# Interleaving the norms of a two-layer decoder trunk with its matmuls, on eight cores

## The chip, the cores and the metric

The kernel runs on the eight cores of one Trainium2 chip. Every core runs the same program on its share of the batch: one new sequence of 2048 tokens and 16 running sequences with 8 new tokens each, 2176 tokens in all. The metric is the device time of the slowest core, in microseconds (us).

Executions come in two states. In the fast state all cores have nearly the same span and clock, and the times of one kernel agree within some 0.3%. In the slow state the cores of one die, sometimes of both, show a lower granted TensorE clock and the time is several per cent longer.

## The reference, cut to what matters

```python
for i in range(DEPTH):                                   # 2 layers
    a = rmsnorm(h, norm_mix[i])
    u, bg, cg, v = split(a @ w_in[i])                    # 4 x 512 columns
    y_pool = pool_mixer(u) ; y_conv = bg * short_conv(cg * v)
    h = h + concat(y_pool, y_conv) @ w_out[i]
    m = rmsnorm(h, norm_mlp[i])
    h = h + relu(m @ w_up[i]) ** 2 @ w_down[i]           # 1024 -> 4096 -> 1024
    gate = sigmoid(rmsnorm(h, norm_ple[i]) @ w_ple_gate[i])
    h = h + gate * (p[i] @ w_ple_proj[i])
return rmsnorm(h, norm_f), new pool states, new conv states
# rmsnorm(x, g) = x * rsqrt(mean(x * x) + 1e-6) * g, in fp32
```

Of the kernel before, what the change touches and what calls it, by code (L numbers as in the profile page):

```python
# [126 lines left out]
def build():  # L127
# [25 lines left out]
    AW = 18944  # L153
    es = ExitStack()
    with es:
        sb = lambda name, shape, dt: es.enter_context(nc.sbuf_tensor(name, shape, dt))
        h = sb("h", [128, KT, NTOK], F32)
        ring = sb("ring", [128, 4, 8, 512], BF16)
        wple = sb("wple", [128, 2, D], BF16)
# [3 lines left out]
        EH = sb("EH", [128, DEPTH, 4, NSEQ * POOL_BUF], F32)  # L163
# [42 lines left out]
        ld_ch = [P.chan(f"ld{i}") for i in range(4)]  # L206
# [50 lines left out]
        SPSTG = 12288  # L257
        SCSTG = 14336
        VSTG = 15360
        vstg = af(VSTG, 128)  # L260
        vstgB = P.abuf()
# [7 lines left out]
        for l in range(DEPTH):  # L269
# [13 lines left out]
            stg = af(SCSTG + l * 512, 512)  # L283
            sB_ = P.abuf()
# [12 lines left out]
        xstgB = [P.abuf() for _ in range(4)]  # L297
        xstg = [af(XSTG + i * 1024, 1024) for i in range(4)]
        for ti, (toff, tw) in enumerate(TILES):
            nsub = tw // 128  # L300
            for s_ in range(nsub):
                src = x_p[toff + s_ * 128: toff + (s_ + 1) * 128, :] if toff < SEQ else x_s
                P.op("sp", lambda e, s_=s_, src=src: e.dma_start(out=xstg[s_], in_=src), writes=[xstgB[s_]], chan=ld_ch[s_])
            if nsub == 4:
                for k in range(KT):
                    b = next_bank()
                    for s_ in range(4):
                        P.op("pe", lambda e, b=b, s_=s_, k=k: e.transpose(out=psum[b][:, s_ * 128:(s_ + 1) * 128], in_=xstg[s_][:, k * 128:(k + 1) * 128], identity=ident[:]),  # L308
                             reads=[xstgB[s_], identB], writes=[psB[b]], signal=(s_ == 3))
# [6 lines left out]
            else:  # L316
                for kh in range(2):
                    b = next_bank()
                    for kk in range(4):
                        k = kh * 4 + kk  # L320
                        P.op("pe", lambda e, b=b, kk=kk, k=k: e.transpose(out=psum[b][:, kk * 128:(kk + 1) * 128], in_=xstg[0][:, k * 128:(k + 1) * 128], identity=ident[:]),
                             reads=[xstgB[0], identB], writes=[psB[b]], signal=(kk == 3))
# [4 lines left out]
        def norm_tile(ti, dst_ap_fn, dstB, gbase):  # L327
            toff, tw = TILES[ti]
            b = next_bank()
            for k in range(KT):  # L330
                q = st["sq"]
                st["sq"] = (q + 1) % 4
                P.op("act", lambda e, q=q, k=k: e.activation(out=sq[:, q, 0:tw], in_=h[:, k, toff:toff + tw], func=AF.Square),  # L333
                     reads=[hB[k][ti]], writes=[sqB[q]])
                P.op("pe", lambda e, q=q, k=k, b=b: e.matmul(psum[b][:, 0:tw], lhsT=ones[:], rhs=sq[:, q, 0:tw], start=(k == 0), stop=(k == KT - 1)),  # L335
                     reads=[sqB[q], onesB], writes=[psB[b]], signal=True)
            n_ = st["norm"]
            st["norm"] = 1 - n_
            P.op("act", lambda e, b=b, n_=n_: e.activation(out=rstd[:, n_, 0:tw], in_=psum[b][:, 0:tw], func=AF.Sqrt, scale=1.0 / D, bias=EPS),  # L339
                 reads=[psB[b]], writes=[rstdB[n_]])  # L340
            P.op("dve", lambda e, n_=n_: e.reciprocal(out=rstd[:, n_, 0:tw], in_=rstd[:, n_, 0:tw]),  # L341
                 reads=[rstdB[n_]], writes=[rstdB[n_]])
            for k in range(KT):
                P.op("dve", lambda e, k=k, n_=n_: e.scalar_tensor_tensor(out=dst_ap_fn(k), in0=h[:, k, toff:toff + tw], scalar=vcol(gbase + k),  # L344
                                                                         in1=rstd[:, n_, 0:tw], op0=ALU.mult, op1=ALU.mult),
                     reads=[hB[k][ti], rstdB[n_], vecB], writes=[dstB[k]])

# [35 lines left out]
        R_OFF = [17408, 17920, 18432]  # L383
# [5 lines left out]
        PT_OFF = 8704  # L389
        G_OFF = [12928, 13440]  # L390
        TMP_OFF = [13952, 14464]
        pT_t = ab(PT_OFF, 2176).rearrange("p (k n) -> p k n", k=2)
        nB = mB
        n_t = m_t
        pTB = [[P.abuf() for _ in TILES] for _ in range(2)]
        gB = [P.abuf() for _ in range(2)]
        tmpB = [P.abuf() for _ in range(2)]
        YFM_OFF = [0, 4096]
        YTM_OFF = [8192, 9216]
        yfmB = [[P.abuf() for _ in range(KT)] for _ in range(2)]  # L400
        ytmB = [P.abuf() for _ in range(2)]

        for l in range(DEPTH):
# [3 lines left out]
            def do_group(l, grp):  # L407
# [39 lines left out]
                for il, ti in enumerate(tl):  # L447
                    o, tw = lo(il)
                    norm_tile(ti, lambda k, o=o, tw=tw: a_t[:, k, o:o + tw], [aB[k][il] for k in range(KT)], V_NMIX + l * 8)

                slot_u = ws_take()
                slot_c = ws_take()
                slot_v = ws_take()
                slot_b = ws_take()
# [7 lines left out]
                def u_chunk(g):  # L462
# [13 lines left out]
                    for il in range(ntl):  # L476
                        b = inproj(slot_u, g, il)
# [72 lines left out]
                def cv_chunk(j):  # L550
# [13 lines left out]
                    for il in range(ntl):  # L564
                        o, tw = lo(il)
                        bc = inproj(slot_c, j, il)
# [4 lines left out]
                        bv = inproj(slot_v, j, il)  # L571
# [31 lines left out]
                def conv_z(j):  # L603
# [5 lines left out]
                    P.op("dve", lambda e: e.tensor_scalar(out=af(Z_OFF, n_), in0=af(coff + 2, n_), scalar1=vcol(cwb + 8), scalar2=vcol(V_CB + l * 4 + j),  # L609
                                                          op0=ALU.mult, op1=ALU.add),  # L610
# [8 lines left out]
                def b_chunk(j):  # L619
                    for il in range(ntl):  # L620
                        o, tw = lo(il)
                        bb = inproj(slot_b, j, il)
                        P.op("dve", lambda e, bb=bb, il=il: e.tensor_tensor(out=dense(mix_t[:, 4 + j, :], il), in0=ctok(Z_OFF, il, 0), in1=pview(bb, il), op=ALU.mult),  # L623
                             reads=[ZB, psB[bb]], writes=[mixB[4 + j][il]])

                u_chunk(0)
                u_chunk(1)
                pool_ew(0)
                pool_state(0)
                u_chunk(2)  # L630
                pool_ew(1)
                pool_state(1)
                u_chunk(3)
                ws_release(slot_u)
                pool_mm(0)
                pool_ew(2)
                pool_state(2)
# [230 lines left out]
```

## The kernel before, where the change touches it

The state `h` lies feature-major in SBUF: 8 blocks of 128 features, each 2176 tokens wide in fp32. Tokens are cut into five tiles, four of 512 prompt tokens and a narrow one of 128 sample tokens. Weights come through a ring of four 1 MB blocks. Each engine is given its work in the order in which the program issues it.

A norm is one function, called for one tile at a time. ScalarE squares a block, TensorE sums it over the features with a matrix of ones, ScalarE takes the square root, and VectorE makes a reciprocal and eight scalings:

```python
def norm_tile(ti, dst_ap_fn, dstB, gbase):
    b = next_bank()
    for k in range(KT):
        P.op("act", ... sq[q] = Square(h[:, k, tile]))
        P.op("pe",  ... matmul(psum[b], lhsT=ones, rhs=sq[q]))
    P.op("act", ... rstd = Sqrt(psum[b] / D + EPS))
    P.op("dve", ... rstd = reciprocal(rstd))
    for k in range(KT):
        P.op("dve", ... dst[k] = h[:, k, tile] * g[k] * rstd)
```

The stages follow one another, each with all its norms ahead of its matmuls:

```python
for ti, (toff, tw) in enumerate(TILES):        # x: 4 staging buffers, loaded, transposed into h
    ...
for l in range(DEPTH):
    for grp in GROUPS:                         # tiles [0, 1], [2, 3], and [4] (the samples)
        for ti in grp: norm_tile(ti, ...)      # mixer norm
        # body: projections u, C, v, B, with pooling and conv between them
        for c in range(KT):                    # output projection, h += ...
            for ti in grp: ...
    for ti in range(5): norm_tile(ti, ...)     # MLP norm of all tiles
    for q in range(4):                         # quarters of the 4096
        for c in range(KT):
            for ti in range(5): ...            # up projection, relu (fp32), square
        for c in range(KT):
            for ti in range(5): ...            # down projection, h += ...
    for ti in range(5): ...                    # load p through 4 buffers, transpose it
    for ti in range(5): norm_tile(ti, ...)     # gate norm of all tiles
    for c in range(KT):
        for ti in range(5): ...                # gate stage: 8 gate matmuls, 2 of p; h += sigmoid * product
for ti in range(5):
    norm_tile(ti, ...)                         # final norm
    ...                                        # transpose back, store through 2 buffers
```

## Time and profile before

| | before |
|---|---|
| times ahead of the prediction | median 2168.81 us of 4 runs (2003.60 to 2258.54) |
| the fast one of them | 2003.60 us |
| profiled run, slowest core | 1998.7 us |
| TensorE busy | 1737.0 us (87%) |
| VectorE, ScalarE busy | 1010.4 us (51%), 466.2 us (23%) |
| mean granted TensorE clock of the slowest core | 0.896 |

The prediction shows the page and the table of stages. In the views PE is TensorE and PEld its weight loads, DVE is VectorE, ACT is ScalarE, POOL is GpSimd and SPq is the queue of SyncE; L730 is a line of the kernel's file. In a timeline a line is the start, the duration, the engine, the source line, the operation, output and inputs, the shape, and how many; in brackets stands the idle time of that engine before it and what ended it. This is TensorE's timeline in the kernel before, where layer 0's gate stage begins with the transposes of p (line L730):

```profile
863.89 1.04 PE L730 MATMUL ps<-ident,pstg 128*128 128x128 f32 x8
868.23 0.30 PE L730 MATMUL ps<-ident,pstg 128*128 128x128 f32 x1 [3.29 <-DMA pstg<-pp]
```

Eight transposes take 1 us and then TensorE waits for the next loads, since a buffer is loaded again only when its transposes are done. The second view is the list of waits of SyncE's queue, which issues the loads of x, in the first 100 us of the kernel before (what waits, for what, us in total, times, longest):

```profile
SPq L797 <- PE ps L308: 48.0, 4, 14.1
...
```

The queue that should issue loads waits 48.0 us for transposes to free a buffer: load and transpose take turns.

### The profile page before, as it was taken

The page shows a single profiled execution, that of the slowest core. Times are in us where ns is not written, and L with a number is a line of the kernel's source. Part 1 is how long each engine was busy: PE and PEld are TensorE (multiplying, and loading weights), DVE is VectorE, ACT ScalarE, POOL GpSimd, SP SyncE. Part 2 cuts the span into 40 slices and gives each one's busy share as a digit, 9 for nine tenths or more (in the row PEclk, how much of TensorE's full clock was granted, in tenths as well). Part 3 has the DMA queues.
Part 4 walks back from the last instruction along what each step waited for, and adds up shares of the span by engine and source line. Part 5 has one row for each costly group of instructions (what it writes and reads, how often), then busy time and mean ns, then how long its engine had stood idle before and what let it go on. Part 6 is the DMA issues. An engine that isn't in the chain of part 4 may idle for free.

```text
span 1998.7 us, 25940 instructions; the slowest of 8 cores (1987.1 to 1998.7 us)
## 1 busy us (share of the span) xinstructions
PE 1737.0 (87%) x8557; PEld 825.4 (41%) x8557; DVE 1010.4 (51%) x1568; ACT 466.2 (23%) x942; POOL 68.4 (3%) x99
## 2 busy tenths in 40 slices
PE   3489887699999999967979887699999999978955
PEld 3234334244444444422424334344444444432433
DVE  1185755744443434429676665744344443429655
ACT  1220311430211203023241311420220303124242
POOL 1000001000000000000000000000000000000000
PEclk8689897699999999977989898689999999977965
DMA  9415246612212212220134326712122122110022
GB/s 199 110 22 85 43 60 97 94 22 43 43 22 43 43 22 42 43 56 0 22 56 66 55 41 100 118 22 43 22 43 43 25 40 43 22 35 1 1 84 95
DMA packets 87887, 103.10 MB, mean 52 GB/s; under 512 B 3790, under 2 KB 81966, under 8 KB 87728
## 3 DMA queue, kind: packets, MB, share of 16 engines
q0 software_dynamic: 76480, 76.81, 26.0%
q1 hardware_dynamic: 11280, 24.64, 3.9%
q8 instruction: 74, 1.21, 0.3%
q14 instruction: 53, 0.43, 0.1%
HBM read 168.61 MB, written 10.10 MB: 89 GB/s over the span
## 4 chain that ended last, share of the span: by engine, by line
PE 73%; DVE 16%; DMA 6%; issue 3%; ACT 1%; SPq 1%; DVEq 0%; ACTq 0%; POOLq 0%
PE ps L353 69%; DVE arena L344 7%; DVE rstd L341 5%; DMA arena<-x_p 2%; PE ps L335 2%; DVE arena L495 1%; DMA ring<-w_out 1%; PE ps L308 1%; DMA pstg<-pp 1%; ACT sq L333 1%; PE ps L730 1%; DVE arena L612 1%; PE ps L773 1%; DMA y_p<-arena 1%; DVE arena L572 0%
## 5 line engine op out<-in xcount | busy, mean ns | idle before, releaser
L353 PE MATMUL ps<-arena,ring 128*128 128x512 bf16 (+1 forms) x7680 | 1506.8, 356 | 56.7 <-DVE arena L344 37.7
L353 PEld LDWEIGHTS ps<-arena,ring 128*128 128x128 bf16 x7680 | 711.0, 101 | 833.4 <-issue 135.3
L698 DVE TENSOR_TENSOR arena<-arena 128x512 bf16<-128x512 f32 (+1 forms) x320 | 189.6, 611 | 278.5 <-ACT arena L696 278.5
L711 DVE TENSOR_TENSOR h<-h,ps 128x512 f32<-128x512 f32 (+1 forms) x320 | 188.9, 607 | 275.6 <-PE ps L353 275.5
L696 ACT ACTIVATE arena<-ps 128x512 f32<-128x512 f32 (+1 forms) x320 | 163.9, 532 | 674.0 <-PE ps L353 652.4
L333 ACT ACTIVATE sq<-h 128x512 bf16<-128x512 f32 (+1 forms) x280 | 131.9, 553 | 163.1 <-PE ps L335 163.1
L344 DVE SCALAR_TENSOR_TENSOR arena<-h,vec,rstd 128x512 bf16<-128x512 f32 (+3 forms) x280 | 166.3, 666 | 4.5 <-PE ps L335 0.9
L335 PE MATMUL ps<-sq,ones 128*128 128x512 bf16 (+1 forms) x280 | 114.6, 461 | 58.4 <-ACT sq L333 49.2
L341 DVE RECIPROCAL rstd<-rstd 128x512 f32<-128x512 f32 (+1 forms) x35 | 100.4, 2869 | 107.8 <-ACT rstd L339 107.8
L672 DVE TENSOR_TENSOR h<-h,ps 128x512 f32<-128x512 f32 (+1 forms) x80 | 48.6, 608 | 82.5 <-PE ps L353 80.3
L335 PEld LDWEIGHTS ps<-sq,ones 128*128 128x128 bf16 x280 | 28.4, 102 | 143.8 <-issue 138.8
L750 ACT ACTIVATE arena<-ps 128x512 f32<-128x512 f32 (+1 forms) x80 | 42.5, 533 | 113.1 <-PE ps L353 86.0
L495 DVE TENSOR_TENSOR arena<-arena 128x1038 f32<-128x1038 f32 (+7 forms) x60 | 60.2, 1003 | 15.8 <-ACT arena L478 12.1
L308 PE MATMUL ps<-ident,arena 128*128 128x128 f32 x128 | 27.1, 381 | 46.5 <-DMA arena<-x_p 46.5
L752 DVE TENSOR_TENSOR arena<-arena,ps 128x512 f32<-128x512 f32 (+1 forms) x80 | 48.5, 606 | 34.3 <-ACT arena L750 25.5
L773 PE MATMUL ps<-ident,arena 128*128 128x128 f32 x136 | 35.2, 410 | 30.0 <-DVE arena L344 30.0
L754 DVE TENSOR_TENSOR h<-h,arena 128x512 f32<-128x512 f32 (+1 forms) x80 | 49.0, 612 | 9.1 <-DVE arena L752 0.9
L314 DVE COPY h<-ps 128x512 f32<-128x512 f32 x16 | 11.1, 692 | 75.2 <-PE ps L308 75.2
L732 ACT ACTIVATE arena<-ps 128x512 bf16<-128x512 f32 (+1 forms) x20 | 10.3, 532 | 150.6 <-PE ps L730 91.7
L353 PE MATMUL ps<-arena,wple 128*128 128x512 bf16 (+1 forms) x160 | 44.4, 360 | 0.7 <-DVE arena L752 0.7
L623 DVE TENSOR_TENSOR arena<-arena,ps 128x512 bf16<-128x512 f32 (+1 forms) x40 | 23.8, 607 | 41.8 <-PE ps L353 40.8
L308 PEld LDWEIGHTS ps<-ident,arena 128*128 128x128 f32 x128 | 23.1, 200 | 50.4 <-issue 50.4
(72 smaller groups left out, 445.3 us busy)
## 6 DMA issues: line engine op xcount, KB each, us to landing
ring<-w_in POOLq DMA_DIRECT2D x24, 1024.0 KB, 10.6
ring<-w_up POOLq DMA_DIRECT2D x16, 1024.0 KB, 8.9
ring<-w_down POOLq DMA_DIRECT2D x16, 1024.0 KB, 8.2
ring<-w_out POOLq DMA_DIRECT2D x12, 1024.0 KB, 10.2
arena<-x_p SPq DMA_DIRECT2D x16, 512.0 KB, 10.4
y_p<-arena SPq DMA_DIRECT2D x16, 512.0 KB, 2.6
pstg<-pp SPq DMA_DIRECT2D x32, 128.0 KB, 2.4
ring<-w_gate POOLq DMA_DIRECT2D x4, 1024.0 KB, 8.4
```

The costliest lines, as they stand in the source:

```text
L308: P.op("pe", lambda e, b=b, s_=s_, k=k: e.transpose(out=psum[b][:, s_ * 128:(s_ + 1) * 128], in_=xstg[s_][:, k * 128:(k + 1) * 128], ident ...
L333: P.op("act", lambda e, q=q, k=k: e.activation(out=sq[:, q, 0:tw], in_=h[:, k, toff:toff + tw], func=AF.Square), reads=[hB[k][ti]], writes ...
L335: P.op("pe", lambda e, q=q, k=k, b=b: e.matmul(psum[b][:, 0:tw], lhsT=ones[:], rhs=sq[:, q, 0:tw], start=(k == 0), stop=(k == KT - 1)), re ...
L341: P.op("dve", lambda e, n_=n_: e.reciprocal(out=rstd[:, n_, 0:tw], in_=rstd[:, n_, 0:tw]), reads=[rstdB[n_]], writes=[rstdB[n_]])
L344: P.op("dve", lambda e, k=k, n_=n_: e.scalar_tensor_tensor(out=dst_ap_fn(k), in0=h[:, k, toff:toff + tw], scalar=vcol(gbase + k), in1=rstd ...
L353: P.op("pe", lambda e, b=b, lap=lap, rap=rap, i=i: e.matmul(psum[b][:, 0:width], lhsT=lap, rhs=rap, start=(i == 0), stop=(i == n - 1)), re ...
L495: P.op("dve", lambda e, doff=doff, src_off=src_off, v=v, sh=sh: e.tensor_tensor(out=af(doff + v, EW - v), in0=af(src_off + v, EW - v), in1 ...
L696: P.op("act", lambda e, b=b, ri=ri, tw=tw: e.activation(out=af(R_OFF[ri], tw), in_=psum[b][:, 0:tw], func=AF.Relu), reads=[psB[b]], writes ...
L698: P.op("dve", lambda e, ri=ri, c=c, toff=toff, tw=tw: e.tensor_tensor(out=f_t[:, c, toff:toff + tw], in0=af(R_OFF[ri], tw), in1=af(R_OFF[r ...
L711: P.op("dve", lambda e, b=b, c=c, toff=toff, tw=tw: e.tensor_tensor(out=h[:, c, toff:toff + tw], in0=h[:, c, toff:toff + tw], in1=psum[b][ ...
L754: P.op("dve", lambda e, gi_=gi_, c=c, toff=toff, tw=tw: e.tensor_tensor(out=h[:, c, toff:toff + tw], in0=h[:, c, toff:toff + tw], in1=af(T ...
L773: P.op("pe", lambda e, b=b, kk=kk, k=k, yoff=yoff, s_=s_: e.transpose(out=psum[b][:, kk * 128:(kk + 1) * 128], in_=af(yoff + k * 512 + s_ ...
```

## The change

Its intent is that no norm stands alone on the path: each one is cut into pieces that are issued between the matmuls of something else. VectorE's nine steps of a norm go into a queue (`defer`), a step or two of which is issued after each matmul unit (`pump`; a unit is the matmuls that sum into one PSUM bank, and in the gate stage the two groups of one output block); `drain` issues what is left when the result is needed. In parts:

1. x is loaded through eight staging buffers, in two alternating sets of four.
2. The mixer norm of the second prompt group: squares and sums beside the first group's last B projections, scalings between its output projections.
3. The sample group's norm goes ahead of the second group's output projection.
4. The first quarter of the up projection goes tile by tile; only the norms of tiles 0 and 1 are summed ahead of it, those of tiles 2 to 4 beside it.
5. p is loaded and transposed behind each tile of that quarter.
6. The last down projection goes tile by tile, with the gate norm of the tile before beside it.
7. The gate stage goes tile by tile. In layer 0 it carries the sums of layer 1's first norm; in layer 1 the final norm, in place in `h`, with transposes and stores a tile later.
8. The first conv term moves from VectorE to ScalarE.
9. The relu result and its square's inputs are bf16, and so is the pool state.

The rest of the diff moves buffers to make room for this.

The core of the diff, with cuts marked:

```diff
-        xstgB = [P.abuf() for _ in range(4)]
+        xstgB = [P.abuf() for _ in range(8)]
+            xo = (ti % 2) * 4
...
-            for grp in GROUPS:
-                do_group(l, grp)
+            gs = [do_group(l, grp) for grp in GROUPS]     # (norm, body, output projection, scalings)
+            gs[0][0]()
+            gs[1][3](gs[0][1](GROUPS[1]["tiles"]))
+            gs[0][2](1)
+            for t_ in GROUPS[1]["tiles"]:
+                drain(t_, V_NMIX + l * 8)
+            gs[1][1]()
+            gs[2][0]()
+            gs[1][2]()
+            gs[2][1]()
+            gs[2][2]()
...
+                if q == 0:
+                    mlp_norm(0)
+                    N = norm_sums(1)
+                    defer(N, ...)
+                    for ti in range(NTL):
+                        drain(ti, V_NMLP + l * 8)
+                        N = norm_begin(ti + 2) if ti + 2 < NTL else None
+                        for c in range(KT):
+                            if N and c >= 4:
+                                norm_sq(N, [2 * (c - 4), 2 * (c - 4) + 1])
+                            up_unit(su, c, ti)
+                            pump(2 if c in (2, 3) else 1)
+                            if N and c >= 4:
+                                norm_mm(N)
...
+                        p_transposes([ti])
...
+                    prev = None                            # last down projection
+                    for ti in [4, 0, 1, 2, 3]:
+                        for c in range(KT):
+                            dn_unit(sd, c, ti)
+                            pump(2)
+                        if prev is not None:
+                            ple_norm(prev)
+                        prev = ti
...
+            for ti in range(NTL):                          # gate stage
+                src = None
+                if last and ti >= 1:
+                    src = ti - 1
+                if not last and ti in (2, 3):
+                    src = ti - 2
...
+                    if N and 1 <= c <= 4:
+                        norm_sq(N, [2 * (c - 1), 2 * (c - 1) + 1])
+                    ple_unit(c, ti)
+                    pump(2 if c > 4 else 1)
...
+                if ti == 0:
+                    ple_norm(3)
```

## The prediction

> **What bounds the kernel now.** I took the views in this order: cores and dies, the page's busy shares, a table of windows cut at the stages, the matmul timeline inside the worst windows, and the groups by shape.
>
> Cores and dies first: in the profiled execution all eight cores took 1987 to 1999 us at a mean clock of 0.895 to 0.904, so no die is held back: the fast state. Of the four timed runs only the 2003.60 us one is of that kind; the others took 2109 to 2259 us. I predict the fast state and compare it with 2003.60.
>
> From the page:
>
> ```profile
> PE 1737.0 (87%) x8557; PEld 825.4 (41%) x8557; DVE 1010.4 (51%) x1568; ACT 466.2 (23%) x942; POOL 68.4 (3%) x99
> ...
> PE   3489887699999999967979887699999999978955
> ...
> PEclk8689897699999999977989898689999999977965
> ...
> DMA  9415246612212212220134326712122122110022
> ```
>
> TensorE is busy 87% of the span, yet both rows dip together, six or seven times: where it waits, its clock is low as well. The table of windows (us, then busy us of each engine, granted clock, DMA share, GB/s) names the dips:
>
> ```profile
> 0.00:91.10 91.10, 34.64 (x161) 28.55 (x161) 11.07 (x16) 14.40 (x25) 7.43 (x29) 0.76 0.79 169
> 91.10:111.40 20.30, 11.93 (x25) 2.49 (x25) 12.89 (x12) 10.69 (x20) 0.00 (x0) 0.58 0.01 2
> 111.40:200.60 89.20, 87.14 (x384) 37.90 (x385) 58.41 (x92) 16.10 (x27) 4.41 (x5) 0.96 0.41 60
> 200.60:217.70 17.10, 9.42 (x25) 2.27 (x24) 13.57 (x13) 8.13 (x15) 0.87 (x1) 0.81 0.40 61
> 217.70:315.40 97.70, 89.97 (x392) 38.90 (x393) 56.80 (x76) 16.22 (x35) 4.38 (x5) 0.95 0.38 55
> 315.40:356.30 40.90, 24.63 (x214) 21.29 (x213) 20.73 (x63) 8.90 (x33) 5.24 (x6) 0.64 0.76 115
> 356.30:397.10 40.80, 28.27 (x75) 7.82 (x73) 36.33 (x40) 20.58 (x44) 0.88 (x1) 0.67 0.60 87
> 397.10:863.90 466.80, 466.68 (x2529) 226.62 (x2529) 190.25 (x326) 80.33 (x157) 13.11 (x15) 0.99 0.23 35
> 863.90:889.50 25.60, 9.44 (x37) 5.50 (x35) 0.77 (x2) 5.80 (x12) 0.87 (x1) 0.62 0.51 108
> 889.50:934.10 44.60, 31.95 (x91) 9.40 (x92) 38.59 (x47) 22.86 (x48) 0.00 (x0) 0.69 0.00 1
> 934.10:1000.30 66.20, 66.20 (x351) 31.68 (x350) 44.91 (x75) 19.53 (x37) 0.87 (x1) 0.97 0.11 17
> 1000.30:1020.80 20.50, 10.71 (x30) 2.51 (x27) 14.78 (x16) 11.73 (x22) 2.32 (x3) 0.73 0.54 84
> ...
> 1902.10:1998.70 96.60, 51.56 (x177) 29.95 (x176) 51.74 (x66) 32.56 (x64) 0.00 (x0) 0.62 0.23 93
> ```
>
> The reader is to see two kinds of row. In the MLP (397 to 864) TensorE is full at clock 0.99: 64 units of 32 wide and 8 narrow matmuls, 7.3 us each, which is 0.216 us for a 512-column matmul and about 0.056 us for a 128-column one. Nothing is to be gained there. In the others TensorE stands beside a norm, a transpose or a load: loading x (0 to 91), the mixer norms (91, 200, 315, 1000), the MLP norms (356), the transposes of p (864), the gate norms (889), the final norm and stores (1902). Inside the MLP norms:
>
> ```profile
> 361.16 3.90 PE L335 MATMUL ps<-sq,ones 128*128 128x512 bf16 x8 [1.46 <-ACT sq L333]
> ...
> 379.24 1.68 PE L335 MATMUL ps<-sq,ones 128*128 128x128 bf16 x8 [2.97 <-ACT sq L333]
> ...
> 391.12 0.38 PE L353 MATMUL ps<-arena,ring 128*128 128x512 bf16 x1 [2.81 <-DVE arena L344]
> ```
>
> Eight sum matmuls take 3.9 us where 1.7 us would do, since each waits for a square from ScalarE (0.53 us apart), and then the projection waits for VectorE's scaling. By shape:
>
> ```profile
> L344 DVE SCALAR_TENSOR_TENSOR arena<-h,vec,rstd 128x512 bf16<-128x512 f32 x192 | 129.3, 746 | 3.3 <-PE ps L335 0.9
> L341 DVE RECIPROCAL rstd<-rstd 128x512 f32<-128x512 f32 x28 | 93.8, 3349 | 104.0 <-ACT rstd L339 104.0
> ```
>
> So one tile's norm is 3.35 us of reciprocal and 8 scalings (back to back 5.39 us, 0.67 each): 8.7 us of VectorE, with TensorE idle.
>
> **What the Trainium skill says.** "TensorE: Matmul & The Clock Gate", section "What's actually happening": the clock gate falls to half rate after an idle window of about 3.4 us and rises after a busy one. The trace agrees: 0.58 to 0.81 in the norm windows, 0.99 in the MLP; hiding a norm also gives its neighbours the full clock. "VectorE: DVE Perf Modes", "The perf-mode tier table": two-tensor operations run at 2x in bf16 and 1x in fp32. The trace has only the fp32 square (0.69 us); no run yet shows the bf16 one, which I estimate at half plus overhead, 0.4 us. "ScalarE: Activation LUTs", "What ACT_TABLE_LOAD costs": a switch costs 1283 ns and about as much drain. The trace shows five loads of 1.28 us, sqrt against sigmoid, and the next instruction directly behind: 1.28 us counts. "DMA: Bandwidth & Descriptors", "Issuing engines are not separate DMA queues": all queues share 16 engines. The trace agrees: while x and weights load together the DMA share is near 1.
>
> **The change, part by part.** No matmul goes away; they move. Savings are the window before minus what stays exposed.
>
> *Loading x.* Four staging buffers become eight, so tile i+1 loads during tile i's transposes. The DMA share 0.79 over 91 us is 72 us of work for 16 engines, much of it the first four weight blocks. Packed, the loads end near 70 us and the last transposes near 75: saves 16.
>
> *Mixer norm of the second prompt group (two layers).* Its squares go beside the first group's last projections, its 18 VectorE steps between the 16 output units (16 x 1.73 = 27.7 us; VectorE needs 16 x 0.69 + 17.4 = 28.4 us, so it ends with the units). Of 17.1 us there remain 16 sums (3.5), 8 projection matmuls (1.7), and 1 of waiting: saves 11 x 2 = 22.
>
> *Sample-group norm.* It goes ahead of the preceding output projection: saves 2.5 x 2 = 5. The wait for w_out at the end of that group stays.
>
> *MLP norms.* The first quarter's up projection goes tile by tile; only tiles 0 and 1 are summed in front. Exposed: sums of 0 (3), of 1 (5), with the square root, reciprocal and scalings of 0 ending near 12.8 us, containing 8 matmuls. To the 40 matmuls that the old 40.8 us held I add the other 32 (5.6) and the hidden sums of tiles 2 to 4 (3.9): 22.3. Saves 18.5 x 2 = 37.
>
> *Transposes of p.* They move behind each tile of that quarter, their loads long landed: 34 x 0.165 = 5.6, plus 1, against 25.6: saves 19 x 2 = 38.
>
> *Gate norms.* The last down projection goes tile by tile with the norm of the tile before. Of 44.6 us, 9.2 is projection. What remains is three sums at 2.5, a narrow one at 0.7, and tile 3's at 4.7, for its squares queue behind the sigmoids: 12.9. Saves 22.5 x 2 = 45.
>
> *Layer 1's first norm.* Its sums (3.5) and reciprocals move into the gate stage; 16 scalings stay: about 12.6 us with 16 matmuls in it, against 20.5 with 8. Saves 5, and 2 go back to table loads and bank waits.
>
> *Final norm and stores.* Scaled in place, transposed and stored beside the next tile. Of 96.6 us stay: three sums (5.2), 96 transposes (15.8), VectorE behind in tile 1 (two norms and its units need 28 us against TensorE's 19, some of it buffered by PSUM: 4), table switches while a sum holds a bank (5), and a tail of 27 (tile 3's scalings, its four stores through two buffers, tile 4's whole norm, the last landing). Saves 40.
>
> *Small ones.* First conv term from VectorE to ScalarE, fewer half-clock stretches in the group bodies: +7; extra waiting for squares in the first group: -2. The bf16 square and state change nothing on the path.
>
> Sum: 16 + 22 + 5 + 37 + 38 + 45 + 3 + 40 + 5 = 211. 1998.7 - 211 = 1788 for the span, and 2 us more for the timed run: 1790 us, 10.7% less.
>
> **The rivals.** *VectorE becomes the bound.* Its 1010 us are moved, not cut (perhaps 90 less for bf16 squares, 16 for conv). In the gate stage a unit gives it 2 x 0.69 plus 0.1 between; with one scaling added that is 2.15 us against 2.16 for TensorE's ten matmuls, and the reciprocal comes on top. If PSUM's eight banks (three units ahead) don't absorb this, each layer's gate stage loses 10 to 15 us and the last one more: 1825. *Weights come late.* Tile by tile both blocks of a pair are held to the end. But the first needs its second block only some 20 us in, and a successor has 59 us of down projection for a landing of about 9; layer 1's first v and b blocks are the doubtful ones. Worst: 1810. *The denser matmuls draw the clock down*, as in the slow runs (5 to 13% longer). Against it: all eight cores ran the MLP together at 0.99 to 1.00. It could make slow executions commoner, and would show in the clocks of a die. *The norm is hidden better than I say*, the half-clock losses around it going too: 1750.
>
> **Range and chances.** The stage sums are firm for the p transposes and the prompt norms, and soft for the load (5), the final stage (20), the gate stage (15) and the weights (10); neglected waits run one way. 1740 to 1855 us. A gain under 2% (40 us) would need four fifths of it to be lost: faster 0.97, same 0.02, slower 0.01.
>
> **What would show it.** TensorE's busy time should fall to some 1600 to 1650 us while the mean clock rises to about 0.96; TensorE should have no idle stretch over 10 us after the first norm but at the two layers' starts, the sample groups and the tail; the last gate unit should end about 27 us before the end; x should be transposed by 75 us; table loads should rise from 5 to about 20. I am wrong if projections wait on VectorE's gate product or scaling within the tile-by-tile stages, on ring loads outside the sample group, or if the clock stays near 0.9.

## The result, and the profile after

| | before | after |
|---|---|---|
| fast runs | 2000.82 to 2003.6 us (7 of 15 runs) | 1775.32 to 1778.05 us (8 of 11) |
| median of all runs | 2074.98 us | 1777.95 us |
| ratio of fast runs, after over before | | 0.8878 (0.8868 to 0.8888) |
| profiled run, slowest core | 1998.7 us | 1776.4 us |
| VectorE, ScalarE busy | 1010.4, 466.2 us | 911.5, 506.4 us |

A ratio is the mean time of one kernel's fast runs over that of the other's of the same rounds, with a 95% interval; so it isn't quite the ratio of the medians above, which mix the states. The kernel became 11.2% faster, with 1790 predicted. The mean granted clock of the slowest core rose from 0.896 to 0.957. Three of the eleven runs after were slow (1920.86 to 1959.16 us).

From the page of the kernel after:

```profile
PE 1635.1 (92%) x8557; PEld 803.5 (45%) x8557; DVE 911.5 (51%) x1544; ACT 506.4 (29%) x982; POOL 68.5 (4%) x99
...
PE   4699895999999999999989988799999999999885
...
PEclk8699997999999999999989998899999999999997
...
```

The same 8557 matmuls took 102 us less of TensorE, since fewer of them ran at half clock, and TensorE's idle time fell from 262 to 141 us. What is left of the dips is at the start, at the two layers' sample groups and at the end.

The table of windows of the kernel after, cut at its own stages (us, then busy us of PE, PEld, DVE, ACT, POOL, then clock, DMA share, GB/s); the rows are x, the first norm, layer 0's up projection of the first quarter with norms and p in it, the rest of the MLP but the last down projection, layer 0's gate stage, and the end:

```profile
0.00:60.60 60.60, 33.03 (x161) 28.86 (x161) 11.07 (x16) 14.13 (x25) 7.43 (x29) 0.83 1.01 232
60.60:80.00 19.40, 11.50 (x25) 2.40 (x24) 12.07 (x11) 10.85 (x21) 0.00 (x0) 0.71 0.52 72
...
303.40:381.80 78.40, 74.55 (x395) 35.75 (x394) 51.18 (x84) 43.17 (x88) 1.75 (x2) 0.97 0.40 68
381.80:735.00 353.20, 353.20 (x1926) 171.98 (x1924) 114.96 (x241) 61.60 (x123) 10.49 (x12) 1.00 0.26 40
...
802.30:891.70 89.40, 84.82 (x432) 38.79 (x431) 69.51 (x96) 46.52 (x77) 1.75 (x2) 0.98 0.12 18
...
1746.50:1776.40 29.90, 12.20 (x63) 9.34 (x60) 17.26 (x31) 7.41 (x18) 0.00 (x0) 0.64 0.39 159
```

Layer 0's gate stage with norms and p took 136.4 us before (clock 0.81) and takes 89.4 now (clock 0.98): a stage that was full of waits now looks like the MLP. The first norm, at 60.6, has nothing to hide behind and is as slow as it was. TensorE's timeline where layer 0's MLP norms begin shows the new order at work:

```profile
303.49 3.43 PE L350 MATMUL ps<-sq,ones 128*128 128x512 bf16 x8
308.39 4.11 PE L350 MATMUL ps<-sq,ones 128*128 128x512 bf16 x8 [1.46 <-ACT sq L340]
...
323.83 0.80 PE L350 MATMUL ps<-sq,ones 128*128 128x512 bf16 x2
324.47 1.89 PE L418 MATMUL ps<-arena,ring 128*128 128x512 bf16 x8
```

The first two tiles' sums still stand alone; from 323.83 on, a pair of sums sits between units of eight projection matmuls and TensorE waits for nothing. By shape, on VectorE:

```profile
L822 DVE TENSOR_TENSOR arena<-arena 128x512 bf16<-128x512 bf16 x256 | 108.4, 424 | 311.4 <-ACT arena L820 311.4
L399 DVE SCALAR_TENSOR_TENSOR arena<-h,vec,rstd 128x512 bf16<-128x512 f32 x144 | 104.5, 747 | 0.4
```

A scaling costs 747 ns as it did (746): the norms' work was moved, not cut. The bf16 square takes 424 ns, close to the prediction's estimate of 0.4 us; the fp32 one took 692.

### Where the time went, stage by stage

Each stage ends where its last weight matmul starts, in both traces; core 3 before, core 1 after.

| stage | before | after | difference |
|---|---|---|---|
| x transposed | 91.1 | 60.6 | -30.5 |
| body of group 2, with its norm (layers 0, 1) | 86.5, 86.2 | 64.2, 64.3 | -22.3, -22.0 |
| body of group 1 (layers 0, 1), now with sums of group 2 | 44.3, 44.3 | 47.5, 47.5 | +3.2, +3.2 |
| sample body, with its norm | 27.1, 26.6 | 22.4, 22.2 | -4.7, -4.5 |
| MLP norms and first up quarter, after also p | 95.9, 96.3 | 78.4, 79.7 | -17.5, -16.7 |
| first down quarter to fourth up quarter | 352.9, 352.9 | 353.2, 353.5 | +0.2, +0.6 |
| last down quarter, after with gate norms | 58.8, 58.8 | 67.4, 67.5 | +8.5, +8.7 |
| gate stage, before with p and norms, layer 0 | 136.4 | 89.4 | -47.0 |
| layer 1's first norm and u projections | 36.2 | 25.4 | -10.8 |
| gate stage, layer 1 (after with the final norm) | 130.6 | 124.6 | -5.9 |
| from there to the end | 96.9 | 29.9 | -67.0 |
| whole span | 1998.7 | 1776.4 | -222.3 |

The rows left out differ by under 1 us each. The predicted sum was -211.

### The profile page after: what moved, and what is told of

Same layout as the page of the kernel before. It is cut to its first block, busy times and chain, and to the rows that moved or that the text cites. A ratio compares the mean times of both kernels' runs of the same rounds, so it can differ in the third digit from the quotient of the medians.

```text
span 1776.4 us, 25497 instructions; the slowest of 8 cores (1764.0 to 1776.4 us)
## 1 busy us (share of the span) xinstructions
PE 1635.1 (92%) x8557; PEld 803.5 (45%) x8557; DVE 911.5 (51%) x1544; ACT 506.4 (29%) x982; POOL 68.5 (4%) x99
## 4 chain that ended last, share of the span: by engine, by line
PE 81%; DVE 8%; DMA 5%; issue 3%; ACT 3%; SPq 1%; DVEq 0%; ACTq 0%; POOLq 0%
PE ps L418 76%; PE ps L350 2%; DVE rstd L364 2%; DMA arena<-x_p 2%; DMA ring<-w_out 2%; ACT sq L340 1%; DVE arena L372 1%; DMA y_p<-arena 1%; DVE arena L565 1%; DVE arena L924 1%; DVE arena L399 1%; DVE h L399 1%; DMA ring<-w_in 1%; PE ps L310 1%; PE ps L938 0%
## 5 line engine op out<-in xcount | busy, mean ns | idle before, releaser
L418 PE MATMUL ps<-arena,ring 128*128 128x512 bf16 (+1 forms) x7680 | 1475.9, 352 | 31.3 <-DMA ring<-w_out 13.6
L418 PEld LDWEIGHTS ps<-arena,ring 128*128 128x128 bf16 x7680 | 702.4, 100 | 771.1 <-issue 65.7
L820 ACT ACTIVATE arena<-ps 128x512 bf16<-128x512 f32 (+1 forms) x320 | 165.5, 532 | 650.7 <-PE ps L418 635.2
L822 DVE TENSOR_TENSOR arena<-arena 128x512 bf16<-128x512 bf16 (+1 forms) x320 | 118.7, 383 | 315.7 <-ACT arena L820 315.5
L350 PE MATMUL ps<-sq,ones 128*128 128x512 bf16 (+1 forms) x280 | 87.7, 375 | 37.3 <-ACT sq L340 30.0
L399 DVE SCALAR_TENSOR_TENSOR arena<-h,vec,rstd 128x512 bf16<-128x512 f32 (+1 forms) x176 | 114.8, 674 | 0.6
L548 ACT ACTIVATE arena<-ps 128x512 f32<-128x512 f32 (+1 forms) x40 | 21.4, 535 | 174.5 <-PE ps L418 164.3
L565 DVE TENSOR_TENSOR arena<-arena 128x1038 f32<-128x1038 f32 (+7 forms) x60 | 60.1, 1002 | 14.4 <-ACT arena L548 10.7
L924 DVE TENSOR_TENSOR arena<-arena,ps 128x512 f32<-128x512 f32 (+1 forms) x80 | 47.9, 599 | 37.7 <-PE ps L418 18.2
L922 ACT ACTIVATE arena<-ps 128x512 f32<-128x512 f32 (+1 forms) x80 | 42.6, 533 | 77.9 <-DVE arena L924 45.0
L418 PE MATMUL ps<-pT,wple 128*128 128x512 bf16 (+1 forms) x160 | 42.6, 348 | 9.7 <-DVE arena L945 5.8
L310 PE MATMUL ps<-ident,arena 128*128 128x128 f32 x128 | 26.5, 387 | 20.3 <-DMA arena<-x_p 20.3
L372 DVE SCALAR_TENSOR_TENSOR arena<-h,vec,rstd 128x512 bf16<-128x512 f32 (+1 forms) x64 | 36.6, 646 | 1.6 <-PE ps L350 1.0
L679 ACT ACTIVATE arena<-arena,vec 128x1024 f32<-128x1024 f32 (+1 forms) x24 | 23.9, 997 | 44.6 <-DVE arena L696 44.6
```

The source lines that it names most:

```text
L350: P.op("pe", lambda e, q=q, k=k, b=b: e.matmul(psum[b][:, 0:tw], lhsT=ones[:], rhs=sq[:, q, 0:tw], start=(k == 0), stop=(k == KT - 1)), re ...
L372: P.op("dve", lambda e, k=k, n_=n_: e.scalar_tensor_tensor(out=dst_ap_fn(k), in0=h[:, k, toff:toff + tw], scalar=vcol(gbase + k), in1=rstd ...
L399: FQ.append((tag, lambda k=k: P.op("dve", lambda e, k=k, n_=n_: e.scalar_tensor_tensor(out=dst_ap_fn(k), in0=h[:, k, toff:toff + tw], scal ...
L418: P.op("pe", lambda e, b=b, lap=lap, rap=rap, i=i: e.matmul(psum[b][:, 0:width], lhsT=lap, rhs=rap, start=(i == 0), stop=(i == n - 1)), re ...
L565: P.op("dve", lambda e, doff=doff, src_off=src_off, v=v, sh=sh: e.tensor_tensor(out=af(doff + v, EW - v), in0=af(src_off + v, EW - v), in1 ...
L820: P.op("act", lambda e, b=b, ri=ri, tw=tw: e.activation(out=ab(R_OFF[ri], 256)[:, 0:tw], in_=psum[b][:, 0:tw], func=AF.Relu), reads=[psB[b ...
```

## The experiments

My theory was that of the prediction: each norm, load or transpose taken off the path gives back its own exposed time, the sum being what the kernel gained. The rivals: that VectorE or late weights take part of it back; that the gain is one of the clock, not of the waits; that the small precision changes did much of it.

Eight runs each undo one part in the kernel after, one puts only the clock right in the kernel before, and three try what the profile after suggests. All gave correct results, and every profiled run was a fast one. The fast runs of the kernel after have a mean of 1777.2 us. The fast runs of before beside the experiments lie between 1998 and 2001 us, those beside the kernel after between 2001 and 2004, so a difference in us below may be off by 2 to 3 us (slowdowns too small, gains too large); the ratios are against before of the same rounds.

### x through four buffers again

```diff
-            xo = (ti % 2) * 4
+            xo = 0
```

> The changed kernel, but with four staging buffers for x again instead of eight. The prediction's step (72 us of DMA work packed to 70 us) gives 16 us back: 1793 us. The stage table of the two traces (x transposed at 91.1 against 60.6 us) gives 30 us back: 1808 us. A rival, that the loads are bound by the 16 DMA engines whatever the staging and the faster start came from elsewhere, gives 0: 1777 us.

Measured: 1801.05 to 1803.14 us, ratio 0.9008 (0.8993 to 0.9022): 25 us slower than after. x was transposed at 89.9 us instead of 60.6, and 4 of those 29 us came back at the later waits for w_out. SyncE's waits, first in the kernel after (0 to 75 us), then with four buffers (0 to 100 us):

```profile
SPq L1021 <- PE ps L310: 30.2, 3, 14.2
...
```

```profile
SPq L1021 <- PE ps L310: 47.5, 4, 13.5
...
```

With four buffers the queue shows the pattern of before. So part 1 is worth about 25 us, not the 16 predicted.

### The second group's norm alone again, between the groups

```diff
-            gs[1][3](gs[0][1](GROUPS[1]["tiles"]))
-            gs[0][2](1)
-            for t_ in GROUPS[1]["tiles"]:
-                drain(t_, V_NMIX + l * 8)
+            gs[0][1]()
+            gs[0][2]()
+            gs[1][0]()
             gs[1][1]()
```

> The changed kernel, but the mixer norm of the second prompt group stands between the groups again, not beside the first group's last projections and its output projection. The prediction's step gives 11 us a layer back: 1799 us. The stage table (22 us less in the second group's body, 3 to 4 more in the first group) gives 18 a layer, if all of it is the norm: 1813 us. A rival, that 7 us a layer of it come from the conv term on ScalarE and not from the norm, gives 11 to 12 a layer here, 1800 us, and the rest in the run with the conv term on VectorE.

Measured: fast runs 1807.32 to 1810.31 us, ratio 0.9037 (0.9018 to 0.9057): 31 us slower, against 22 predicted. Per layer the second body grew by 21.6 and 20.7 us, and the first one shrank by 4.1, having no sums to carry. Where the extra lies shows in the timeline of this experiment at the end of the norm, where VectorE scales the second tile and TensorE runs the first eight matmuls that need it:

```profile
186.26 5.39 DVE L372 SCALAR_TENSOR_TENSOR arena<-h,vec,rstd 128x512 bf16<-128x512 f32 x8
187.15 5.22 PE L418 MATMUL ps<-arena,ring 128*128 128x512 bf16 x8 [3.74 <-DVE arena L372]
```

and in its windows there and right behind:

```profile
188.80:192.10 3.30, 2.91 (x6) 0.55 (x6) 3.00 (x7) 0.00 (x0) 0.00 (x0) 0.50 0.00 0
192.20:195.50 3.30, 3.30 (x9) 1.15 (x8) 2.21 (x3) 0.60 (x1) 0.00 (x0) 0.50 0.00 0
195.60:199.00 3.40, 3.40 (x18) 1.61 (x17) 1.03 (x3) 1.34 (x3) 0.00 (x0) 1.00 0.00 0
```

In the kernel after, in the same projections with no norm ahead of them:

```profile
159.80 20.67 PE L418 MATMUL ps<-arena,ring 128*128 128x512 bf16 x95
```

There a matmul takes 0.22 us. In the experiment the eight take 5.0 us to the start of the next: one for each scaling, 0.66 us apart, with waits so short that the timeline joins them in one row. The next eight, from 192.2 on, wait for nothing and take 0.43 us each at the half clock of 0.50; from 195.6 on the clock is 1.00. At full clock each eight would take 8 x 0.217 = 1.7 us. So behind the last wait that the timeline lists, 5.0 us a layer are lost, 3.3 to VectorE's scalings and 1.7 to the half clock, and the prediction's step counted neither.

### First conv term on VectorE again

```diff
-  P.op("act", ... activation(out=z, in_=cv, func=Identity, scale=w2, bias=b))
+  P.op("dve", ... tensor_scalar(out=z, in0=cv, scalar1=w2, scalar2=b, op0=mult, op1=add))
```

> The changed kernel, but the first conv term is computed on VectorE again. If the 7 us a layer that the second group's body lost beyond its norm come from this term: 1789 to 1793 us. If they come from the full clock and the missing VectorE backlog behind the norm: 1776 to 1780 us.

Measured: fast runs 1777.38 to 1779.12 us, ratio 0.8891 (0.8875 to 0.8907): 1 us slower, which the interval doesn't tell from none. The second group's body grew by 2.6 us in each layer, but the time did not follow: most of it was given back at later waits.

### The square from fp32 again

```diff
-  activation(out=relu_bf16[ri], in_=psum[b], func=Relu)
+  activation(out=relu_f32[ri], in_=psum[b], func=Relu)     # and the square reads fp32
```

> The changed kernel, but relu's result is kept and squared in fp32 again (0.69 instead of 0.42 us a wide tile, some 70 us more of VectorE's busy time). Theory: VectorE has room in the MLP, so 1777 us within 3. Rival: VectorE is near its bound in the tile-by-tile quarter, where it also scales: 1785 to 1800 us.

Measured: fast runs 1777.03 to 1778.14 us, ratio 0.8887 (0.8871 to 0.8903): no difference. The fp32 squares again took 0.69 us each on VectorE, and no stage moved by more than about 2 us. So the 71 us of VectorE time that the bf16 squares save (189.6 us busy in the kernel before, 118.7 after, wide and narrow ones together) lie off the path.

### All five MLP norms in front of the first up quarter

```diff
-                    mlp_norm(0)
-                    N = norm_sums(1)
-                    defer(N, ...)
+                    for ti in range(NTL):
+                        mlp_norm(ti)
...
-                        N = norm_begin(ti + 2) if ti + 2 < NTL else None
+                        N = None
```

> The changed kernel, but all five MLP norms stand in front of the first quarter again (which stays tile by tile). The prediction's step gives 18.5 us a layer back: 1814 us. Counted more closely for this very edit, the sums of all tiles are paced by VectorE's 8.7 us a tile and TensorE starts tile 0 some 25 us in, having lost 17 to 18 instead of 7.6 us: 10 a layer, 1797 us. A rival, that VectorE merely works later and nothing is gained, gives 1777 us.

Measured: two quiet runs at 1792.13 and 1793.37 us, one at 1816.57 (counted as fast, with clocks down to 0.940) and a slow one at 2058.41; ratio 0.9028 (0.8929 to 0.9127), wide because of the third run. The quiet runs are 15 us slower than after. In the profiled run, at 1792.13, the stage was 11.2 and 9.9 us longer in the two layers, and some of that came back later. So the interleaved sums are worth about 8 to 10 us a layer. The stage is still shorter than before, although it also holds p's transposes: 89.6 against 95.9 us. The tile-by-tile order gains by itself, as the units of tile 0 need only tile 0's scalings and run while VectorE scales the others.

### Gate norms in front of the gate stage

```diff
-                        if prev is not None:
-                            ple_norm(prev)
-                        prev = ti
                     ws_release(sd[0])
                     ws_release(sd[1])
+                    for ti in range(NTL):
+                        ple_norm(ti)
+                        drain(ti, V_NPLE + l * 8)
...
-                if ti == 0:
-                    ple_norm(3)
```

> The changed kernel, but the five gate norms run between the last down projection and the gate stage instead of beside the down projection. The prediction's step gives up to 22.5 us a layer back (1822 us) where the first gate units also wait as before; with tile-by-tile units behind the fronted norms, 15 a layer: 1807 us, or a few us less if VectorE's backlog in the gate stage of layer 1 goes away with it (1802 us). A rival, that this backlog costs as much as the hiding gains: under 1790 us.

Measured: 1810.0 to 1812.23 us, ratio 0.9059 (0.9043 to 0.9075): 34 us slower. Layer 0's last down projection fell by 7.6 us and its gate stage rose by 26.8; in layer 1 it was -7.8 and +24.6. So hiding them is worth about 17 to 19 us a layer.

### p transposed at the gate stage again

```diff
-                        p_transposes([ti])
...
             P.stage_barrier()
+            p_transposes(range(NTL))
             sg = [ws_take(), ws_take()]
```

> The changed kernel, but the transposes of p stand in front of the gate stage again. The prediction's step gives 19 us a layer back: 1815 us. A rival, that their loads would overlap the norms' scalings now and only the TensorE work and a clock drop remain: 5 to 8 a layer, 1790 us.

Measured: fast runs 1809.67 to 1814.68 us, ratio 0.9066 (0.9048 to 0.9083): 35 us slower, 18 a layer, with 19 predicted. The gate stages took 25.1 and 21.6 us more and the first up quarters 2.2 and 3.3 less. The loads are the same; in the kernel after they land under 79 us of matmuls, and TensorE's transposes of p wait 0.1 us in all, where they waited 25.3.

### The final norm after the last gate unit

```diff
-                if last and ti >= 1:
-                    src = ti - 1
...
-                N = norm_sums(NTL - 1)
-                final_scale(N)
-                (drain and store what is left)
+                for ti in range(NTL):
+                    final_scale(norm_sums(ti))
+                    drain(ti, V_NF)
+                    final_out(ti, list(range(TILES[ti][1] // 128)))
```

> The changed kernel, but the final norm, transposes and stores come after the last gate unit again. The prediction's step gives 40 us back: 1817 us. The stage table (the last layer's gate stage and tail together took 154.5 us, of which some 84 would be the gate stage alone and 97 the old tail) gives 26: 1803 us; the difference would be VectorE's backlog and the table loads in that stage, sized too small in the prediction.

Measured: 1801.38 to 1803.63 us, ratio 0.9018 (0.9002 to 0.9034): 26 us slower, not 40. Layer 1's gate stage took 42.4 us less and the stretch behind it 68.0 more. So the tail fell about as predicted, and the pieces cost more inside the gate stage than I gave them (30 us). Two things held them up. The waits in the kernel after, from 1625 us to the end:

```profile
ACT arena L942 <- DMA y_p<-arena: 27.2, 8, 9.1
...
ACT arena L922 <- DVE arena L924: 18.7, 7, 7.7
...
PE ps L350 <- ACT sq L340: 17.8, 7, 5.7
```

ScalarE copies rows to be stored (L942) into one of two buffers, and waited 27.2 us for stores to leave them. It also waited for VectorE (L924, the gate product), which at 1672.76 took a reciprocal of 3.35 us and then eight scalings in one piece of 5.39. Everything behind on ScalarE waits with it, also the squares that TensorE needs:

```profile
1682.29 0.60 ACT L922 ACTIVATE arena<-ps 128x512 f32<-128x512 f32 x1 [7.67 <-DVE arena L924]
...
1683.55 1.10 PE L350 MATMUL ps<-sq,ones 128*128 128x512 bf16 x2 [5.16 <-ACT sq L340]
```

### The clock alone: the kernel before with dummy matmuls in its norms

```diff
 # in norm_tile, after each sum matmul
+                dummy(1)                          # ones x a constant block, into a bank that nobody reads
+            dummy(16 if tw == 512 else 4)         # behind the last sum, ahead of the projections
```

> The kernel before, unchanged but for dummy matmuls: one behind each of a norm's eight sum matmuls and sixteen behind the last (four for the narrow tile), into a bank that nobody reads, so that TensorE stays busy while ScalarE and VectorE do the norm. Theory: the half clock inside a norm costs nothing, since ScalarE and VectorE pace it, and only the first 10 us behind it, still at half clock, do (some 4 us at each first group, 6 at each second, a few more at the sample groups and gate stages): 1970 to 1985 us against 2001. Rival: the half clock is a cause of its own and most of the 102 us by which TensorE's busy time fell are on the path: 1930 us or less.

Measured: fast runs 2006.94, 2007.73 and 2011.4 us, ratio to before 1.0047 (1.0027 to 1.0067). In the profiled runs the clocks of the cores rose from 0.895 to 0.904 before to 0.945 to 0.949, almost those of the kernel after, and the time did not fall. My expectation, 1970 to 1985 us, was wrong. The windows of layer 0's second prompt group; before, at the second tile's scalings, and with dummies, the norm and these scalings:

```profile
217.90:221.20 3.30, 2.91 (x6) 0.52 (x5) 3.30 (x6) 0.00 (x0) 0.00 (x0) 0.50 0.00 0
```

```profile
200.70:218.00 17.30, 15.90 (x74) 7.01 (x72) 13.39 (x13) 8.25 (x15) 0.87 (x1) 1.00 0.45 62
218.20:221.40 3.20, 1.88 (x5) 0.45 (x5) 3.20 (x6) 0.00 (x0) 0.00 (x0) 1.00 0.00 0
```

Inside the norm the clock is 1.00 instead of 0.81 and nothing is gained, as TensorE isn't what the norm waits for. Behind it TensorE follows the second tile's scalings in both runs, at half clock before and at full clock until 221.4 with dummies, and again nothing is gained: the scalings end 21.8 us after the norm's start before and 22.0 with dummies. My expectation had put all 10 us behind the norm down to the half clock. A stretch at half clock behind the scalings is there in both runs (0.50 from 221.3 to 224.7 us, and from 221.5 to 224.8 with dummies), as the dummies all stand ahead of the first projections. The body's length came out the same, 86.5 us. So a high clock where TensorE waits for others buys nothing. What the short stretch behind the scalings costs (1.7 us in the second experiment) this run doesn't measure.

### Six output buffers instead of two

```diff
-        st_ch = [P.chan(f"st{i}") for i in range(2)]
+        st_ch = [P.chan(f"st{i}") for i in range(6)]
...
-        YTM_OFF = [14848, 15872]
+        YTM_OFF = [10752, 11776, 12800, 13824, 14848, 15872]
...
-                    ti_ = st["y"] % 2
+                    ti_ = st["y"] % 6
```

> The changed kernel with six instead of two buffers (and semaphores) for the transposed output rows. ScalarE waits 27 us for stores to land in the last stage and its sigmoids and squares queue behind. If that is what the prediction missed in the final stage: 1765 to 1769 us. If VectorE's bursts (reciprocal and eight scalings, 8.7 us in one piece) are: 1775 to 1778 us.

Measured: 1767.38 to 1769.48 us, ratio 0.8846 (0.8831 to 0.8861): 9 us faster than after by the means, 6 by the ratios. Layer 1's gate stage lost 3.4 us and the end 4.4. In the waits from 1620 us on, ScalarE no longer waits for stores:

```profile
ACT arena L942 <- PE ps L938: 16.5, 10, 4.3
```

So some 6 to 9 of the 14 us missing in the last step came from two buffers. Part of the wait only moved: ScalarE waits 24.1 us for VectorE's gate product there, 18.7 in the kernel after.

### The narrow tile first in the last gate stage

```diff
-            for ti in range(NTL):
+            seq = [4, 0, 1, 2, 3] if last else list(range(NTL))
+            for n_, ti in enumerate(seq):
```

> The changed kernel, but the last layer's gate stage takes the narrow tile first and the wide tile 3 last. The narrow tile's eight units (4.4 us) took 22 us beside tile 3's norm and tile 2's transposes. If they were too short to hide these, the stage shortens by some 10 to 15 us although the tail then holds a wide tile: 1763 to 1768 us. If the tail of a wide tile costs what the narrow one hid: 1774 to 1780 us.

The reason for it is TensorE's timeline of the kernel after, in the narrow tile's units, which close the stage:

```profile
1737.69 1.10 PE L350 MATMUL ps<-sq,ones 128*128 128x512 bf16 x2 [2.35 <-ACT sq L340]
...
1750.00 0.27 PE L418 MATMUL ps<-pT,wple 128*128 128x128 bf16 x2 [3.26 <-DVE arena L945]
```

A narrow unit's ten matmuls are done in 0.7 us (1728.41 to 1729.14), and beside it go sums and stores of a wide tile; the eight units took 22 us (1728.4 to 1750.3). Measured: fast runs 1774.38 and 1776.47 us, ratio 0.888 (0.8859 to 0.8902), and two slow ones: no change. The gate stage lost 10.7 us and the tail gained 10.0, since now a wide tile's norm and four stores are left for the end. The wait moved.

### Together, with the first norm started while x loads

```diff
+            if ti < 2:                                   # in the x loop, behind tile ti's transposes
+                norm_tile(ti, ...)                       # layer 0's first norm
...
-            gs[0][0]()
+            if l > 0:
+                gs[0][0]()
```

with the two edits before.

> The changed kernel with three things more: six output buffers, the narrow tile first in the last gate stage, and the first layer's mixer norm of tiles 0 and 1 done right behind their transposes, while the later tiles of x load (the first body then starts with its norm done; the norm took 20 us of which the sums, 3.5 us, stay). Sum of the three if they add: 15 for the norm, 8 for the buffers, 10 for the order: 1744 us. If VectorE's scalings hold up the copies of the later tiles of x, half of the first: 1752 us.

Measured: fast runs 1749.81 to 1753.25 us, and two slow ones; ratio 0.8764 (0.8747 to 0.8781), 1.3% better than the kernel after (0.8764 / 0.8878). The first norm went under the load of x: the end of the first body is 22 us earlier, and x is transposed only 1.8 us later. So the first norm gave 22 us where 15 were expected; the other two edits together gave 5 where 18 were (the last gate stage and the tail took 149.5 us, 154.5 in the kernel after). This is the fastest version.

## Why the prediction was right, step by step

The time was predicted at 1790 us and came out at 1777: the mechanism held, and the bounds named for TensorE held too: busy 1635.1 us (1600 to 1650 predicted), clock 0.957 (0.96), 21 table loads in place of 5 (20 predicted), the last gate unit ending 26 us before the end (27), and no idle stretch of TensorE over 7.6 us after the first norm (10). But the sum is better than its terms, since misses in both directions cancelled. The "measured" column is from the undoing experiment where there is one, and from the stage table where not; parts share stages, so that the column is good to a few us.

| step of the prediction | predicted | measured |
|---|---|---|
| loading x | 16 | 25 (the stage: 30) |
| second group's norm, two layers | 22 | 31 |
| sample norm, two layers | 5 | 8 (stages) |
| MLP norms, two layers | 37 | some 40 (stages) |
| transposes of p, two layers | 38 | 35 |
| gate norms, two layers | 45 | 34 |
| layer 1's first norm | 3 | some 4 (stages) |
| final norm and stores | 40 | 26 |
| small ones | 5 | 1 (the conv term; the half clock is in the rows above) |

The 40 are the 34.2 us of the two up stages, with the 5.5 us put back that p adds to them (2.2 and 3.3 in the experiment on p). The 8 are the 9.2 us of the sample bodies less 1.6 by which the output projections ahead of them grew. The 4 are the 10.8 us at layer 1's start less 7.1 us that its sums and table loads add to layer 0's gate stage (89.3 us, against 82.2 for layer 1's in the run with the final norm behind, which carries neither). The prediction counted 3.5 us of sums there and 2 of table loads and bank waits; its own figures for this step give 6, not 5, before these 2.

*Loading x.* The step "packed, the loads end near 70 us" was mis-sized: x was transposed at 60.6. The amount of transfer was judged right (a DMA share of 0.79 over 91.1 us before, 1.01 over 60.6 after, and 0.52 in the 19 us behind), but I let x land last among all of it. In the kernel after x lands within the first 61 us and part of the weights' traffic after it.

*Second group's norm.* The mechanism was right and the size too small. The step took a window of 17.1 us that ends at 217.7, the last wait that the timeline lists. But eight more matmuls follow the second tile's scalings (3.3 us lost in the second experiment) and the eight behind these run at half clock (1.7 us): 5.0 us a layer, of which only the half clock was named, in the general 7 us. Both are gone in the kernel after, where those projections run at 0.22 us each.

*MLP norms.* Close: 18.5 us a layer predicted, about 20 seen. The run with all norms in front splits it: 8 to 10 us are the interleaved sums, and the rest is the order by tiles alone, which already takes that stage from 95.9 us with no p in it to 89.6 with p.

*p and the sample norm.* p came out as worked out: loads long landed, 18 us a layer.

*Gate norms and the final stage.* Here I was too hopeful. For the gate norms 17 us a layer came out instead of 22.5. The mis-sized term is the 12.9 us that were to remain: the pieces take 8.5 us in the last down projection and 8.6 in the gate stage, 17.1 in all. (The 8.6 are layer 1's gate stage in the run with the final norm behind, 82.2 us, less an estimated 73.6 for its matmuls at 0.216 and 0.056 us each.) In the final stage the failed step is "VectorE behind in tile 1 ... 4" and "table switches while a sum holds a bank (5)", as part of 30 us that the pieces were to add inside the stage; they add 42. Two buffers for stores cost 6 to 9 us of it. The narrow tile is too short to hide a wide tile's norm: the stage lost 10.7 us when it was moved to the front, though the tail then took them back. The rest, with ScalarE waiting for VectorE's burst of nine steps, is seen in the trace but not removed by a run.

*The rivals.* "VectorE becomes the bound" did not come true in layer 0: its gate stage ran at 84.8 us busy of 89.4 with the clock at 0.98. In the last gate stage a burst on VectorE did stall ScalarE, and through its squares TensorE, up to 5.2 us at a time; for the gate product itself TensorE waited 0.5 us in all. "Weights come late" did not come true: TensorE's waits for the ring were two on w_out, 13.6 us in all, in the sample groups, where they were expected to stay. "The denser matmuls draw the clock down" did not come true in fast runs: the MLP ran at 1.00. Slow runs were 3 of 11 after and 8 of 15 before, too few to say more than that they did not become commoner here. "The norm is hidden better than I say" came true for the first half of the kernel and not for the last stage.

*What stays open.* The single undoings with a result of their own add to some 170 us (25 + 31 + 1 + 0 + 15 + 34 + 35 + 26 = 167; by the ratios some 180) of the 225 that the fast runs gained. The stage table gives some 30 more to the order by tiles of the first up quarter (some 9 us a layer), the sample norm and layer 1's first norm; none of these was undone by itself, so their share is read from the stages, not shown by a run. The remaining 15 to 30 us are not assigned.

## What to carry to other kernels

A serial norm between matmul stages costs more than the waits that a timeline lists: the matmuls behind it follow its last scalings one by one (0.66 us apart here, where 0.22 would do) and then run at half clock for a time (3.4 us in the second experiment); cut it into pieces, let the units that need only the first tile start first, and issue a piece beside each unit, small enough that no engine is held for several us (one burst of VectorE held ScalarE for 7.67 us here). Look for the clock's dips as symptoms: filling them with useless work raised the clock by 0.05 and gained nothing. Check what paces each piece once it is hidden: the last stage gave 26 us of the 40 that it promised, and two store buffers took 6 to 9 of what was missing; and moving work off one end of a stage can simply put it at the other.

## What the Trainium skill lacked or had wrong

- "TensorE: Matmul & The Clock Gate", "What's actually happening": it says that full clock comes after at least one busy window of about 3.4 us, but not how busy a window must be. In the second experiment the window of 188.8 to 192.1, with a matmul every 0.66 us, did not end the half clock (a matmul without waits took 0.43 us at that clock); the next one, 192.2 to 195.5, without waits, did. In the kernel before with dummies a matmul every 0.66 us, at full clock (0.22 us each), was followed by the half clock from 221.4 on.
- The same page has no word on what a higher clock is worth where another engine sets the pace: with dummy matmuls the clock of the slowest core went from 0.90 to 0.945, and the ratio of the times was 1.0047.
- "ScalarE: Activation LUTs", "What ACT_TABLE_LOAD costs": it gives 1283 ns and about 1380 ns of drain for a switch. The load took 1283 ns here, but no drain beside it: in the kernel after a load of 1.28 us began at 1688.35, 0.14 us after the work ahead of it ended, and the square root began at 1689.64, directly behind. With 21 loads the page's drain would be, as an estimate, 29 us more of ScalarE.
